# The even mixer's long convolution moved from VectorE to TensorE, and the S5 tables built in 48 steps between the weight chunks

## Chip, cores and metric

The kernel runs on one core of a Trainium2 chip. The metric is the device time of one execution in microseconds (us); less is better. Engines are TensorE (PE in the profile, its weight loads PEld), VectorE (DVE), ScalarE (ACT), GpSimd (POOL) and SyncE (SP), which here only issues transfers.

## What is computed

The reference is a network on one sequence of 512 positions with 1024 features, all in float32. A first block has an even mixer and an odd mixer, each behind a norm, and a final norm; a second block has an S5 state-space mixer, a gated unit, two MLPs and an attention. The change is in the even mixer, and in the tables which the S5 mixer uses much later:

```
p = rmsnorm(h) @ w_in
a_val, a_glu, a_gate, b_val, b_gate = split(p)
u = a_val * sigmoid(a_glu)
u = causal_depthwise_conv(u, conv_w, conv_b)
u = silu(layernorm(u))
ya = u * silu(a_gate)
yb = (multiscale_pool_diff(b_val) @ pool_w + pool_b) * pool_scale * silu(b_gate)
h = h + concat(ya, yb) @ w_out
```

The depthwise convolution has 31 taps over the positions, with weights of its own for each of the 1024 channels. The S5 tables are products of powers of a complex number for each of 64 groups by 64 states with the matrices B and C, and sines and cosines of 64 angles each.

## The kernel before

Activations lie with the features on the 128 partitions: eight tiles of 128 x 512. Weights come in chunks. `queue_w` lists them in the order of use (58 for the even mixer, 512 KB each); `prep` (line 259) loads one into one of two `raw` buffers through SP (line 264), copies it on ScalarE to `hi`, a rounded float32 (line 266), and takes the difference `lo = raw - hi` (line 268), on GpSimd if the chunk's number is in `on_pool`, which holds all numbers below 107, or else on VectorE. There are three buffers of `hi` and of `lo`, and `get_w` prepares up to three chunks ahead. `mm3` (lines 284 to 286) multiplies in three matmuls, hi by hi, hi by lo, lo by hi, so one chunk is 24 matmuls of 512 columns. `mtile` does one chunk into a PSUM bank. The elementwise helpers are recorded at one line each: `act` 225, `tt` 228, `stt` 240, `ts` 243.

`even` (line 420) runs so. The inputs are squared and split; the first four chunks multiply the input before it is normalized, while the norm is worked out (column sums, line 344; a Newton iteration on four numbers, `rsqrt_col`; a matmul that spreads them, line 373). Then for each of eight tiles `mtile` gives value and gate, and `us[c]` is value times sigmoid (as tanh). The convolution (lines 496 to 516) takes two tiles at a time in a PSUM bank each: ScalarE does the tap of one position back with the bias, VectorE the 30 others, one `stt` each over up to 512 columns, at low priority (`later(4000)`). `csum` adds up the eight results. `pooled` (line 522) and the loop behind it do the pooling half: eight chunks for values and eight for gates, with VectorE adding shifted copies. Then the mean of the convolution (a matmul of ones on `csum`, line 561), the squares, eight output chunks for the pooling half, eight chunks for the gate `a_gate` with the LayerNorm's sums and rsqrt in between (`LNC`, `LNS`: at which chunk and step), then `normed`, `gated` and `halved` for each tile and eight output chunks for the convolution half.

The S5 tables are made by the generator `tables` (line 893), eight turns, one for each `ft`; all eight are called at once at the second gated tile (`extra`, `TS = (8, 0, 0)`) at low priority (`TLATE = 8000`), so that they fill gaps. One turn has, for each half q, small products on GpSimd (line 931 on) and wide ones (`cmul`, line 955), matmuls of 128 x 32 weights on 128 columns into a quarter of a bank's partitions (lines 970, 972), transposes (line 978), copies and stores to DRAM (`tS`, `tO`, lines 982 and 989), and later `tM` (line 1001) and the sines (`reduce_angle`, `tR`, line 1017). `eng2`, which makes the output tables and the angles, is GpSimd for the first four turns and VectorE for the others.

The Tile framework orders each engine's instructions by priority in a timeline that it works out itself; `high_priority(offset)` moves some forward (`HOT = 9000` for the tables' matmuls), `later(n)` back, and `after()` binds an instruction behind the last one written for its engine. Each engine runs its instructions in order, and SP and ScalarE issue transfers from their own queues in the same order.

## Time and profile before

| | us |
|---|---|
| median of 3 runs (1898.36 to 1901.58) | 1899.34 |
| the profiled execution | 1902.89 |
| its span, first to last instruction | 1901.1 |
| TensorE busy in it | 1758.7 |
| VectorE busy in it | 1259.9 |
| ScalarE busy in it | 749.7 |
| GpSimd busy in it | 571.0 |
| even mixer: start of the span to the first matmul of the odd mixer | 446.87 |

The page cuts the span into 40 slices of 47.5 us and gives each engine's busy share in tenths. TensorE's matmuls are pipelined and the ends of their records are modelled, so a matmul's record is longer than the distance to the next one: the starts tell the pace. "x" counts records.

### The profile page before, as it was taken

The numbers are of one execution on the slowest core, as the hardware profiler recorded it, in microseconds if no ns is written. First come the engines' busy times: TensorE is split into PE (matmuls) and PEld (weight loads), VectorE is DVE, ScalarE is ACT, GpSimd is POOL, SyncE is SP. The second block draws the span as 40 slices with busy tenths as digits, with TensorE's granted clock in tenths as the row PEclk, the third lists the DMA queues.
The fourth block names the chain that finished last, engine by engine and source line by source line (L and its number), as shares of the span: only waits on it lengthen the run. The fifth ranks groups of instructions, "written<-read, shape, count | busy, mean of one in ns | idle before, by whom it ended". The sixth has DMA issues, their size and how long they took to land.

```text
span 1901.1 us, 23182 instructions
## 1 busy us (share of the span) xinstructions
PE 1758.7 (93%) x8530; PEld 1425.8 (75%) x8530; DVE 1259.9 (66%) x1940; ACT 749.7 (39%) x1274; POOL 571.0 (30%) x606
## 2 busy tenths in 40 slices
PE   6998989799988797699999999998999999999997
PEld 5776767567766676587888888887778888888886
DVE  8999999975788768844542344578776642244456
ACT  3334332443445543223432342334665542233234
POOL 4789877684556653300000000023000000000002
PEclk7999989889998998899999999999999999999998
DMA  4233233333121468723233223233111223322322
GB/s 151 78 117 99 87 106 122 110 89 102 64 75 64 125 207 297 227 78 105 100 100 95 94 100 100 92 110 113 51 44 56 93 96 100 100 91 98 100 90 93
DMA packets 104289, 200.57 MB, mean 106 GB/s; under 512 B 26736, under 2 KB 57072, under 8 KB 104176
## 3 DMA queue, kind: packets, MB, share of 16 engines
q1 hardware_dynamic: 96496, 182.41, 30.0%
q0 software_dynamic: 2640, 8.65, 1.4%
q10 hardware_dynamic: 5040, 8.04, 1.2%
q8 instruction: 67, 1.10, 0.2%
q14 instruction: 46, 0.38, 0.1%
HBM read 176.38 MB, written 22.02 MB: 104 GB/s over the span
## 4 chain that ended last, share of the span: by engine, by line
PE 57%; DVE 23%; issue 6%; DMA 5%; POOL 4%; ACT 3%; SPq 1%; ACTq 0%; DVEq 0%; POOLq 0%
PE mm L284 17%; PE mm L285 16%; PE mm L286 16%; DVE cv L240 7%; POOL lo L228 2%; DVE pl L228 1%; DMA raw<-in_w_in_odd 1%; PE pv L1519 1%; SPq L1085 1%; DVE srr L228 1%; ACT hi L225 1%; DVE e L733 1%; PE sc L284 1%; PE sc L285 1%; PE sc L286 1%
## 5 line engine op out<-in xcount | busy, mean ns | idle before, releaser
L225 ACT ACTIVATE hi<-raw 128x1024 fp32r<-128x1024 f32 (+1 forms) x280 | 292.1, 1045 | 661.3 <-PE mm L285 533.7
L228 DVE TENSOR_TENSOR lo<-raw,hi 128x1024 fp32r<-128x1024 f32 (+1 forms) x185 | 226.7, 1226 | 407.0 <-ACT hi L225 403.6
L286 PE MATMUL mm<-xg,lo 128*128 128x512 f32 x924 | 364.8, 395 | 6.4 <-POOL lo L228 6.4
L284 PE MATMUL mm<-xg,hi 128*128 128x512 f32 x924 | 365.4, 397 | 1.5 <-ACT xs L225 1.5
L285 PE MATMUL mm<-xg,hi 128*128 128x512 f32 x924 | 363.8, 395 | 0.0
L1333 POOL DMA_DIRECT2D pj<-proj x16 | 8.7, 547 | 1023.8 <-DVE t L240 784.0
L228 POOL TENSOR_TENSOR lo<-raw,hi 128x1024 fp32r<-128x1024 f32 (+1 forms) x95 | 231.3, 2436 | 134.5 <-ACT hi L225 125.1
L284 PE MATMUL mm<-hid,hi 128*128 128x512 f32 (+1 forms) x648 | 250.7, 387 | 1.8 <-DVE t L228 1.8
L285 PE MATMUL mm<-hid,hi 128*128 128x512 f32 (+1 forms) x648 | 250.3, 387 | 0.0
L286 PE MATMUL mm<-hid,lo 128*128 128x512 f32 (+1 forms) x648 | 250.1, 386 | 0.0
L286 PEld LDWEIGHTS mm<-xg,lo 128*128 128x128 f32 x924 | 175.9, 190 | 45.1 <-POOL lo L228 7.9
L284 PEld LDWEIGHTS mm<-xg,hi 128*128 128x128 f32 x924 | 176.1, 191 | 40.4 <-ACT xs L225 1.9
L285 PEld LDWEIGHTS mm<-xg,hi 128*128 128x128 f32 x924 | 175.9, 190 | 38.2 <-issue 1.2
L240 DVE SCALAR_TENSOR_TENSOR cv<-b,hw,cv 128x510 f32<-128x510 f32 (+28 forms) x232 | 158.8, 726 | 0.0
L284 PEld LDWEIGHTS mm<-hid,hi 128*128 128x128 f32 x648 | 121.7, 188 | 26.6 <-DVE t L228 2.0
L286 PEld LDWEIGHTS mm<-hid,lo 128*128 128x128 f32 x648 | 121.7, 188 | 24.7
L285 PEld LDWEIGHTS mm<-hid,hi 128*128 128x128 f32 x648 | 121.7, 188 | 24.6
L284 PE MATMUL mm<-y,hi 128*128 128x512 f32 x192 | 77.7, 405 | 10.5 <-ACT y L225 9.3
L286 PE MATMUL mm<-y,lo 128*128 128x512 f32 x192 | 75.7, 395 | 1.7 <-POOL lo L228 1.7
L285 PE MATMUL mm<-big,hi 128*128 128x512 f32 x160 | 68.5, 429 | 8.6 <-DVE big L240 7.6
L285 PE MATMUL mm<-y,hi 128*128 128x512 f32 x192 | 75.7, 394 | 0.0
L284 PE MATMUL mm<-big,hi 128*128 128x512 f32 x160 | 65.7, 429 | 10.1 <-DVE gt L240 5.8
(467 smaller groups left out, 3140.6 us busy)
## 6 DMA issues: line engine op xcount, KB each, us to landing
raw<-in_w_up SPq DMA_DIRECT2D x64, 512.0 KB
raw<-in_w_down SPq DMA_DIRECT2D x64, 512.0 KB
raw<-in_w_in_even SPq DMA_DIRECT2D x40, 512.0 KB
raw<-in_w_in_odd SPq DMA_DIRECT2D x24, 512.0 KB
raw<-in_w_out_even SPq DMA_DIRECT2D x16, 512.0 KB
raw<-in_w_glu SPq DMA_DIRECT2D x16, 512.0 KB
raw<-in_w_gate SPq DMA_DIRECT2D x16, 512.0 KB
raw<-in_w_out_odd SPq DMA_DIRECT2D x16, 384.0 KB
```

Source lines behind the costliest of these rows:

```text
L225: self.nc.scalar.activation(out=out, in_=in_, func=func, scale=scale, bias=bias)
L228: (eng or self.nc.vector).tensor_tensor(out=out, in0=a, in1=b, op=op)
L240: self.nc.vector.scalar_tensor_tensor(out=out, in0=a, scalar=s, in1=b, op0=op0, op1=op1)
L284: mm(out, hi[:, sl], xh, start=start, stop=False)
L285: mm(out, hi[:, sl], xl, start=False, stop=False)
L286: mm(out, lo[:, sl], xh, start=False, stop=stop)
L733: nc.vector.tensor_tensor_scan(out=y, data0=u[:, k], data1=x[:, k], initial=0.0, op0=ALU.mult, op1=ALU.add)
L1085: nc.sync.dma_start(out=M0[:, 128 * g:128 * g + 128], in_=bass.AP(k0.tensor, k0.offset + 4096 * g, [[16, 8], [256, 16], [1, 128]]))
L1333: self.nc.gpsimd.dma_start(out=p, in_=pj[m])
L1519: mm(o, l, r[:, w], start=n == 0, stop=n == 6 * nk - 1)
```

## The change

The convolution becomes matmuls. The channels of a tile are 16 groups of 8, and a row of positions is cut into four phases (position modulo 4). `u` is written phase by phase and stored to DRAM (`phases`), and four loads bring it back in a layout `z` that has 8 channels x 4 phases on 32 partitions, once for each of four shifts of up to three steps: 128 partitions, 16 groups of 128 columns. `taps` loads a 128 x 192 table of halved taps and spreads it, on VectorE, over the channels with a mask `own` into three 128 x 512 tiles of weights, 32 columns for each group and each of three longer shifts. `convolve` multiplies: 4 x 3 x 4 matmuls a tile, four column groups in turn, which gives 32 outputs each; ScalarE adds the bias, the result goes to DRAM and comes back with the phases in order as `conv[c]`. `step(c)` runs after tile c's gating: the sum of tile c - 4, the convolution of tile c - 3, the taps of tile c - 2; steps 8 to 11 stand in the first two pool groups.

The tables' generator now yields 48 times. `tick`, called after each weight chunk (52 times), takes one step at a small lag of priority (`TLATE = 300`), and TensorE's part of a step is put off by two ticks (`TLAG = 2`) and bound behind the chunk before it. Odd turns work on VectorE, even ones on GpSimd, the output tables always on GpSimd, the angles always on VectorE; `tS` and `tR` are stored from ScalarE's queue. The PSUM banks `tab` and `cv` become two and one. Of the even chunks' numbers from 6 to 57 the `lo` difference goes to VectorE. The norm, mean and LayerNorm steps move (`EPOS`, `MU`, `LNC`, `LNS`). The `big` tiles are taken in quarters of a four times larger tile.

```diff
-    NACT, CACT = range(8), range(0, 8, 2)
-    LNC, LNS = (6, 3), (7, 2)
-    YA, LNP, SQB, TS = 3, 2, 3, (8, 0, 0)
-    SQX, EPOS = (0, 2, 5), (0, 4)
+    MU, LNC, LNS = 2, (4, 0), (5, 0)
+    YA, LNP, SQB = 3, 2, 3
+    SQX, EPOS = (0, 2, 5), (4, 4)
+    TAPP = ()
     BOOST = 400
-    on_pool = frozenset(range(107))
+    on_pool = frozenset(n for n in range(107) if n > 57 or n % 2 or n < 6)
...
-        more(2, range(self.EPOS[0], self.EPOS[1]))
+        more(2, range(self.EPOS[0], 8))
+        more(3, range(self.EPOS[1]))
         with self.after():
             rb = self.spread_bank(rc)
...
-        us = []
+        conv, csum, ready, done = [None] * 8, self.L("b", 9), {}, []
+        def phases(c, u):
+            cu = self.dram.tile([128, T], F32, name=f"cu{c}")
+            nc.sync.dma_start(out=cu, in_=u)
+            z = self.L("big", 4, F32, (128, 4 * T)).rearrange("p (g t) -> p g t", g=16)
+            nc.gpsimd.memset(z[0:96, :, 0:3], 0.0)
+            for a in range(4):
+                src = bass.AP(cu.tensor, cu.offset, [[128, 32], [4096, 16], [1, 125 + a]])
+                nc.sync.dma_start(out=z[32 * a:32 * a + 32, :, 3 - a:128], in_=src)
+            ready[c] = z
+        def taps(c):
+            wd = self.L("wd", 2, F32, (128, 192))
+            nc.sync.dma_start(out=wd, in_=self.I["conv_a_w"][c])
+            self.act(wd, wd, AF.Copy, scale=0.5)
+            ws = []
+            for k in range(3):
+                w = self.L(*(("sq", self.SQB), ("gt", 3))[c % 2])
+                self.tt(w.rearrange("p (g d o) -> p g d o", g=16, d=8),
+                        wd[:, 64 * k:64 * k + 64].rearrange("p (g o) -> p g o", g=16).unsqueeze(2).to_broadcast([128, 16, 8, 4]),
+                        self.own.unsqueeze(1).unsqueeze(3).to_broadcast([128, 16, 8, 4]), ALU.mult, nc.gpsimd if c in self.TAPP else None)
+                ws.append(w)
+            ready[c] = ready[c], ws
+        def convolve(c):
+            z, ws = ready.pop(c)
+            y = self.bank("cv")
+            for q in range(4):
+                for k in range(3):
+                    for g in range(4):
+                        w = ws[k][:, 32 * (4 * q + g):32 * (4 * q + g) + 32]
+                        with self.after():
+                            nc.tensor.matmul(y[32 * g:32 * g + 32, 128 * q + 4 * k:128 * q + 128], w, z[:, 4 * q + g, 0:128 - 4 * k],
+                                             start=k == 0, stop=k == 2, tile_position=(0, 32 * g))
+            o = self.L("v", 2)
+            for q in range(4):
+                self.act(o[:, 128 * q:128 * q + 128], y[:, 128 * q:128 * q + 128], AF.Identity, bias=self.V("conv_a_b", 4 * c + q))
+            cy = self.dram.tile([T, 128], F32, name=f"cy{c}")
+            nc.scalar.dma_start(out=cy.rearrange("(q p) t -> p q t", p=128), in_=o.rearrange("p (q t) -> p q t", q=4))
+            conv[c] = self.L("b", 9)
+            nc.sync.dma_start(out=conv[c], in_=cy.rearrange("(h p) t -> h (p t)", p=4))
+            done.append(c)
+        def summed():
+            for c in done[len(done) - 1:]:
+                if c:
+                    self.add(csum, csum if c > 1 else conv[0], conv[c])
+        def step(c):
+            if 2 < c < 12:
+                summed()
+            if 2 < c < 11:
+                convolve(c - 3)
+            if 1 < c < 10:
+                taps(c - 2)
         for c in range(8):
             th = self.L("th", 2)
-            u = self.L("b", 9)
+            u = self.L("pl", 3)
             if c < self.EAGER:
                 pv, pg = first[2 * c:2 * c + 2]
                 self.mul(th, pg, rs)
                 pg = th
-                self.mul(u, pv, rs)
-                pv = u
+                m = self.L("v", 2)
+                self.mul(m, pv, rs)
+                pv = m
             else:
                 pv = self.mtile(xg)
+                self.tick()
                 pg = self.mtile(xg)
+                self.tick()
             self.act(th, pg, AF.Tanh, scale=0.5)
-            self.stt(u, th, 1.0, pv, ALU.add, ALU.mult)
-            us.append(u)
+            p4 = lambda x: x.rearrange("p (t o) -> p t o", o=4)
+            self.stt(u.rearrange("p (o t) -> p t o", o=4), p4(th), 1.0, p4(pv), ALU.add, ALU.mult)
+            phases(c, u)
             if c == self.EAGER - 1:
                 if self.BN == 2:
                     behind_norm()
                 extra()
-        csum = None
...
-        conv = us
+            step(c)
...
+                step(8 + 2 * g + c)
...
         for m in range(8):
             o = self.mtile(yb)
+            self.tick()
             self.add(h[m], o, h[m])
+            if m == self.MU:
+                mu = self.bank("st")
+                with self.after():
+                    nc.tensor.matmul(mu, self.ones, csum, start=True, stop=True)
+                for c in range(9):
...
         def gated(c):
-            self.mul(conv[c], conv[c], ga[c])
+            v, ga[c] = ga[c], self.L("d", 6)
+            p4 = lambda x: x.rearrange("p (t o) -> p t o", o=4)
+            self.mul(p4(ga[c]), conv[c].rearrange("p (o t) -> p t o", o=4), p4(v))
...
+        while self.behind or next(self.ft, 0) is None:
+            self.tick()
...
-    SHARED, OWN, HOT, TLATE = 4, 8, 9000, 8000
+    HOT, TLATE, TLAG = 9000, 300, 2
+    def tick(self):
+        self.ticks += 1
+        while self.behind and self.behind[0][0] <= self.ticks:
+            self.behind.pop(0)[1]()
+        if self.ft is not None:
+            with self.later(self.TLATE):
+                next(self.ft, None)
...
-            eng = nc.gpsimd if ft < self.OWN else nc.vector
-            eng2 = nc.gpsimd if ft < self.SHARED else nc.vector
+            eng, eng2 = nc.vector if ft % 2 else nc.gpsimd, nc.gpsimd
...
+                def products(q=q, wr=wr, wi=wi, cbr=cbr, cbi=cbi, kt=kt, tS=tS):
+                    if q == 0:
+                        kt.append(self.bank("tab"))
+                    for w, cb in ((wr, cbr), (wi, cbi)):
+                        for a in range(2):
+                            p4 = 2 * q + a
+                            with self.after():
+                                nc.tensor.matmul(kt[0][32 * p4:32 * p4 + 32, 0:128], cb[:, a], fl(w)[:, a], start=w is wr, stop=w is wi, tile_position=(0, 32 * p4))
+                    tp = self.bank("tab")
+                    for k, w in enumerate((wr, wi)):
+                        for a in range(2):
+                            with self.after():
+                                nc.tensor.transpose(out=tp[:, 256 * k + 128 * a:256 * k + 128 * a + 128], in_=fl(w)[:, a], identity=self.ident)
+                    sv = Q("sv", 512)
+                    nc.scalar.dma_start(out=tS.rearrange("p (k a n) -> p k a n", k=2, a=2)[:, :, q], in_=sv.rearrange("p (k n) -> p k n", k=2))
+                late(products)
+                yield
...
+                late(stored)
...
-                self.tt(ang.rearrange("p (a c) -> p a c", a=2), c3(self.chunk), s3(th8), ALU.mult, eng2)
-                r = self.reduce_angle(ang, 128, eng2, "sr")
+                self.tt(ang.rearrange("p (a c) -> p a c", a=2), c3(self.chunk), s3(th8), ALU.mult)
+                r = self.reduce_angle(ang, 128, None, "sr")
...
+                nc.scalar.dma_start(out=tR.rearrange("p (k a n) -> p k a n", k=2, a=2)[:, :, q], in_=rt)
+                yield
...
-        with self.phase(mm=4, tab=1, cv=2):
+        with self.phase(mm=4, tab=2, cv=1):
```

Two small unused tiles (`pad`, `gap`) shift later addresses in SBUF.

## Rows read from the trace of the kernel before

**Rows 1.** The page: an engine's busy time, one engine's slices, the chain.
```profile
PE 1758.7 (93%) x8530; PEld 1425.8 (75%) x8530; DVE 1259.9 (66%) x1940; ACT 749.7 (39%) x1274; POOL 571.0 (30%) x606
...
DVE  8999999975788768844542344578776642244456
...
PE 57%; DVE 23%; issue 6%; DMA 5%; POOL 4%; ACT 3%; SPq 1%; ACTq 0%; DVEq 0%; POOLq 0%
PE mm L284 17%; PE mm L285 16%; PE mm L286 16%; DVE cv L240 7%; POOL lo L228 2%; DVE pl L228 1%; DMA raw<-in_w_in_odd 1%; PE pv L1519 1%; SPq L1085 1%; DVE srr L228 1%; ACT hi L225 1%; DVE e L733 1%; PE sc L284 1%; PE sc L285 1%; PE sc L286 1%
```

**Rows 2.** Sums by stage: busy us (records) of each engine, clock, DMA share, GB/s.
```profile
725.00:750.00 25.00, 17.84 (x170) 14.66 (x170) 21.77 (x38) 7.58 (x11) 13.73 (x11) 0.77 0.99 356
0.00:447.00 447.00, 386.40 (x1675) 299.30 (x1676) 422.28 (x723) 169.93 (x350) 339.69 (x440) 0.93 0.35 108
...
55.00:447.00 392.00, 346.90 (x1516) 267.87 (x1515) 374.51 (x578) 149.40 (x312) 313.52 (x402) 0.94 0.34 104
```

**Rows 3.** TensorE's timeline: start, duration, line, what it multiplies, shapes.
```profile
54.85 0.63 PE L284 MATMUL mm<-xg,hi 128*128 128x512 f32 x2
...
352.80 0.39 PE L284 MATMUL mm<-xg,hi 128*128 128x512 f32 x1
...
358.26 0.39 PE L284 MATMUL mm<-xg,hi 128*128 128x512 f32 x1
...
386.50 0.42 PE L970 MATMUL tab<-tq_wr,cbr 128*32 128x128 f32 x4 [0.37 <-ACT tq_kq L225]
386.72 0.42 PE L972 MATMUL tab<-tq_wi,cbi 128*32 128x128 f32 x4
...
446.87 0.47 PE L284 MATMUL mm<-xg,hi 128*128 128x512 f32 x1
```

**Rows 4.** TensorE's waits, 50 to 450 us: total, times, longest (14 entries).
```profile
PE st L561 <- DVE b L228: 6.4, 1, 6.4
PE st L373 <- DVE rs_s L240: 6.0, 1, 6.0
PE mm L284 <- DVE gt L240: 5.8, 1, 5.8
PE tab L996 <- ACT tq_sv L225: 4.9, 4, 1.9
```

**Rows 5.** VectorE, 0 to 447 us: instructions on tiles cv, srr and srk, in turn.
```profile
0.00:447.00 447.00, 164.23 (x240) 0.93 0.35 108
...
0.00:447.00 447.00, 23.04 (x32) 0.93 0.35 108
...
0.00:447.00 447.00, 14.91 (x40) 0.93 0.35 108
```

**Rows 6.** VectorE by line and shape: 0 to 447, last row 447 to 900.
```profile
L228 DVE TENSOR_TENSOR d<-v,d 128x512 fp32r<-128x512 f32 x8 | 14.1, 1758 | 0.0
...
L228 DVE TENSOR_TENSOR h<-mm,h 128x512 f32<-128x512 f32 x16 | 10.8, 681 | 4.9 <-PE mm L286 4.9
...
L228 DVE TENSOR_TENSOR tq_wi<-tq_wi,tq_u 128x256 f32<-128x256 f32 x8 | 6.0, 754 | 0.1
...
L228 DVE TENSOR_TENSOR tq_ang<-ctile,sbr 128x128 f32<-128x128 f32 x8 | 2.7, 338 | 1.1 <-ACT tq_rt L225 1.1
...
L228 DVE TENSOR_TENSOR lo<-raw,hi 128x1024 fp32r<-128x1024 f32 x21 | 25.6, 1222 | 44.2 <-ACT hi L225 44.1
```

**Rows 7.** GpSimd by line and shape, 0 to 415 us.
```profile
L228 POOL TENSOR_TENSOR lo<-raw,hi 128x1024 fp32r<-128x1024 f32 x55 | 135.0, 2456 | 62.4 <-ACT hi L225 60.6 <-issue 1.6
L228 POOL TENSOR_TENSOR tq_wi<-tq_wi,tq_u 128x256 f32<-128x256 f32 x23 | 20.1, 875 | 0.7
```

**Rows 8.** SP: issue (ns min/median/max), its wait; transfers: count, size, landing.
```profile
L989 SPq DMA_DIRECT2D tO<-tq_wr x32: 577/600/642, 86.8 to 444.0; - x32
...
SPq L264 <- POOL lo L228: 166.6, 41, 15.4
...
U<-du POOLq DMA_DIRECT2D x8, 256.0 KB, 4.7
```

More of the change, by code (lines that the diff above doesn't have):

```diff
@@ L136, in host_layout @@
     c.add("half", np.repeat(np.repeat(np.eye(2, dtype=np.float32)[::-1], 64, axis=0), 16, axis=1))
+    c.add("own", np.tile(np.repeat(np.eye(8, dtype=np.float32), 4, axis=0), (4, 1)))
     c.add("not0", np.repeat((np.arange(64) > 0).astype(np.float32)[None], 128, axis=0))
@@ L173, in __init__ @@
         self.p_s = P("small", 4)
+        P("pad", 1).tile([128, 16], F32, name="pad")
         self.p_raw = P("raw", 2)
@@ L404, in consts @@
         self.tab, self.U, self.acc12 = [], [], []
+        self.ft, self.behind, self.ticks = None, [], 0
     def load_x(self, ps=None):
@@ L431, in even @@
                 self.act(q, h[k], AF.Square)
-            xu.append(self.split(h[k], self.LR("big", 16), self.V("g_even", k)))
+            xu.append(self.split(h[k], [self.quarter() for _ in range(2)], self.V("g_even", k)))
             if k == 0:
@@ L467, in even @@
             self.act(rs, rb, AF.Copy)
-        more(2, range(self.EPOS[1], 8))
-        more(3, range(8))
+        more(3, range(self.EPOS[1], 8))
         xg = []
@@ L590, in even @@
                     self.mm3(pg, w, k, xg[k], k == 0, k == 7)
-            g = self.L("big", 16)
+            self.tick()
+            g = self.quarter(F32)
             self.act(g, pg, AF.Silu)
@@ L609, in even @@
                         f(k)
-        tables(2)
         n = self.YA
@@ L898, in tables @@
         nc.gpsimd.memset(z, 0.0)
-        cbr, cbi = (self.L(n, 1, F32, (128, 2, 32)) for n in ("cbr", "cbi"))
-        nc.gpsimd.memset(cbr, 0.0)
-        nc.gpsimd.memset(cbi, 0.0)
+        cbs = [[self.L(f"cb{n}{q}", 1, F32, (128, 2, 32)) for n in "ri"] for q in range(2)]
+        for cb in cbs:
+            for t in cb:
+                nc.gpsimd.memset(t, 0.0)
         cr, ci, pr, pi, m8, th8 = small
@@ L960, in cmul @@
                     self.tt(out, out, u, op, eng)
-                wr, wi = F("wr", 2), F("wi", 2)
+                wr, wi = F("wr", 3), F("wi", 3)
                 cmul(wr, pw(pr, 0), hb(bbr), pw(pi, 0), hb(bbi), ALU.subtract, eng)
                 cmul(wi, pw(pr, 0), hb(bbi), pw(pi, 0), hb(bbr), ALU.add, eng)
-                for a in range(2):
-                    p4 = 2 * q + a
-                    o = kt[32 * p4:32 * p4 + 32, 0:128]
-                    with self.tc.high_priority(offset=self.HOT):
-                        nc.tensor.matmul(o, cbr[:, a], fl(wr)[:, a], start=True, stop=False, tile_position=(0, 32 * p4))
-                    with self.tc.high_priority(offset=self.HOT):
-                        nc.tensor.matmul(o, cbi[:, a], fl(wi)[:, a], start=False, stop=True, tile_position=(0, 32 * p4))
@@ new lines, in tables, with inside, turned @@
+                late(stored)
+                if q == 1:
+                    def inside(ft=ft, kt=kt, tM=tM):
+                        ks = Q("ks", 128)
+                        self.act(ks, kt[0][:, 0:128], AF.Copy)
+                        self.stt(ks[:, 0:16], self.eye16, dg[:, ft:ft + 1], ks[:, 0:16], ALU.mult, ALU.add)
+                        def turned():
+                            kp = self.bank("tab")
+                            with self.after():
+                                nc.tensor.transpose(out=kp[:, 0:128], in_=ks, identity=self.ident)
+                            kq = Q("kq", 128)
+                            self.act(kq, kp[:, 0:128], AF.Copy)
+                            for j in range(8):
+                                nc.sync.dma_start(out=tM[:, :, 8 + j].rearrange("g h m -> h g m"), in_=kq[16 * j:16 * j + 16].rearrange("p (g m) -> p g m", g=8))
+                        self.behind.insert(0, (self.ticks + 1, turned))
+                    late(inside)
@@ L1685, in behind_norm @@
                         self.small = next(small)
-            def tables(i):
-                if on("s5"):
-                    with self.later(self.TLATE if i == 0 else 0), self.after(mybir.EngineType.DVE) if i else nullcontext():
-                        for _ in range(self.TS[i]):
-                            next(self.ft)
-            h = self.even(h, behind_norm, extra, tables)
+            h = self.even(h, behind_norm, extra)
         if on("odd"):
```

139 lines of the change are left out of this document (50 added, 89 removed).

## The prediction

> **What bounds the kernel now.** I read the page first, from its engine line to its slices and its chain [rows 1]. TensorE is busy for 93% of the span, but VectorE's slices stand at 8 or 9 through the first eight of forty, and nowhere later for so long. In the chain of waits 23% is VectorE, and the largest VectorE entry, 7%, is the convolution line. So the even mixer, the first quarter, is a stage in which VectorE paces TensorE. The sums by stage say it in time [rows 2]: from 0 to 447 us VectorE is busy for 422 us, TensorE's records cover 386, GpSimd 340, ScalarE 170. Outside the even mixer the change touches nothing, so only this stage counts.
>
> Then the pace of TensorE itself. Its timeline [rows 3] has the first matmul on normalized activations at 54.85 and the first of the odd mixer at 446.87: 392 us. At full clock 24 matmuls, one weight chunk, go from 352.80 to 358.26: 5.46 us. Of the 58 chunks of queue_even four are done before 54.85, so 54 x 5.46 = 295 us are dense matmuls and 392 - 295 = 97 us are something else. The list of TensorE's waits [rows 4] has 14 entries between 50 and 450, 45 us in all; the rows show the three longest, which are the LayerNorm sum, the rsqrt behind it and a pool gate, all owed by VectorE, then the first of six entries for the S5 tables, which together take 17.6 us. About 19 us more are the small matmuls of tables and norms (estimate: sixteen half tables, each with eight product records in two rounds of 0.22 us [rows 3] and transposes for as long again, and 5 us for the norms). The other 33 us are matmuls at the lower clock, which follow each stop: granted clock 0.94 over 55 to 447 [rows 2].
>
> **The change, part by part.** *Convolution off VectorE.* Its 240 instructions are 164 us of VectorE [rows 5]. All go.
>
> *Convolution onto TensorE.* Per tile 4 x 3 x 4 = 48 matmuls in F32, K = 128, 32 columns of weights, 120 to 128 columns of data; 384 in all. The nearest rows are the table products, of the very same shape [rows 3]: each matmul leaves two records, and at 386.50 four records, two matmuls in different column groups, are through in 0.22 us, when the next four begin. The change puts four groups side by side. If all four share as the two do, a tile is 12 x 0.22 = 2.6 us and the sum 21; if only pairs share, 42; if each ran alone, 84, which the rows exclude for two groups. I take 21, since in the rows the second group costs nothing beside the first, and keep 42 as the upper end. The Trainium skill, TensorEngine Tiling (Array Packing), Theoretical Speedup, gives weights of up to 32 columns up to four times the speed; by it too the sum would be 21.
>
> *What feeds it.* Per tile VectorE gains three 512-wide tensor_tensor that spread the taps. Bounds: 0.68 us, the add on a PSUM operand that never meets GpSimd, and 1.76 us, the same size on SBUF while GpSimd works [rows 6]; I take 0.9, as GpSimd will be less busy: 24 x 0.9 = 22 us. ScalarE gains some 20 us of bias and scaling on 170 busy of 447, hidden in its gaps. GpSimd gains eight small memsets, hidden likewise. SP gains seven transfers a tile, 56 x about 0.6 us of issue [rows 8], but gives the 32 stores of tS and tR to ScalarE's queue, at the same price 19 us there, still within ScalarE's idle time. The bytes are 1.9 MB a tile, 15 MB in all, beside 108 GB/s x 447 us = 48 MB now; from 725 to 750 us the core moved 356 GB/s [rows 2]. Each step of the convolution uses what was stored at least a tile earlier, some 11 us of dense matmuls, so I cost latency at nothing; the cover is the three-tile lag.
>
> *Weight halves.* 26 of the even chunks' subtractions move from GpSimd, 2.46 us each [rows 7], to VectorE, 1.22 us as in the odd mixer [rows 6]: +32 us VectorE, -64 GpSimd.
>
> *Tables.* All angle reductions go to VectorE: the eight it does now cost 23.0 + 14.9 + 2.7 = 41 us [rows 5, 6], so +41. Of the output tables it gives up 48 operations of 256 columns, at most 0.75 us and at least the 0.34 of a 128-wide product [rows 6]; I take 0.6, so -29. For odd tiles it takes over 8 x (6 small at 0.3 and 6 wide at 0.6) = 43 us, with four pairs that scale B 46. GpSimd sheds these at 0.88 for a wide one [rows 7], 8 x (6 x 0.3 + 6 x 0.88) = 57 us; the angles it sheds and the output tables it gains are about equal.
>
> *Order.* The table steps lose the early place that HOT gave their matmuls, and the convolution's products come between them. Their 64 stores of tO and 64 of tM stay on SP, in the same number, those of tO two ticks later, so that SP no longer stands before an unfinished one; the weight loads behind them gain by that. At the start the column sums of the first norm move behind four more steps of 3 matmuls, 2.7 us, and as many fewer follow them: between 3 us lost, if rsqrt sets the end of the first norm, and 3 gained, if the eight steps now cover it; I take nothing. The mean moves behind the third output tile and the LayerNorm's rsqrt to gate chunks 4 and 5, so three chunks, 16 us, cover the normalizing instead of three quarters of one.
>
> *Sum on VectorE:* 422 - 164 + 22 + 32 + 41 - 29 + 46 = 370 us, and less as GpSimd falls from 340 to some 220 and holds it up less often: 345 to 370. That is below the 390 us at which TensorE can end at best (54.85 + 295 + 19 + 21). **TensorE becomes the bound.**
>
> *What is regained.* The wait for the LayerNorm sum goes, since the convolution ends in the second pool group, some 25 chunks earlier. The gate wait goes with VectorE's queue. Of the rsqrt wait (6.0 us, now covered by one chunk) I keep 3. Of the tables' 17.6 I keep 4: their matmuls now stand in TensorE's order two ticks, 11 us, behind the vector work. With 5 for weights, 12 of 45 us stay. The low-clock part shrinks alike, 33 to 9. The odd mixer starts without table work beside it: 3. In all 33 + 24 + 3 = 60 us back. Paid: 21 for the convolution and 10 for new waits of TensorE in its now fixed order (bounds 0 and 17.6, what tables cost today; taken near the middle). Behind a late product stands every dense matmul, as nothing may pass it. Net -29 us.
>
> The profiled execution took 1902.9 us (span 1901.1); the median of the runs is 1899.3, 3.6 less. 1902.9 - 29 = 1874, and by the median **1870 us**.
>
> **The rivals.**
> - *Cleaner than I think:* all waits go and only the floor of 390 us stays: 447 - 390 = 57 back, 1843. Against it: VectorE at 345 to 370 of 390 leaves little slack. 7%.
> - *Pairs only:* the four groups share two by two: 21 us more, 1891. For it: no row has more than two groups. 11%.
> - *VectorE remains the bound:* its new tensor_tensor pay contended prices, taps 24 x 1.76 = 42 and halves 26 x 1.9 = 50, so 408 us; with the 25 us of idling that it has now, 433: 14 back, 1885. It decides if GpSimd stays above some 300 us. 8%.
> - *Not the convolution:* the waits come from weights and queues; only sum, gate and rsqrt go, 18 us and 13 of slow clock, which the 31 paid eat up: 1899. Against it: weights are not among the long waits of TensorE [rows 4]. 5%.
> - *Slower, by SP's queue:* SP is in order. For each tile it must wait until u has landed in DRAM before it may issue the four loads, and again until the convolution's output has landed; a 256 KB transfer that reads DRAM back takes 4.7 us elsewhere [rows 8]. The weight loads stand behind. If a hold, store and issue together, reaches 9 us (two such landings), it outruns the 5.46 us of one chunk in reserve by 3.5, sixteen times: 56 us lost, 27 slower, 1926. It decides when a hold exceeds about one chunk. Against it: SP already waits 167 us for free raw buffers [rows 8], so loads run ahead. 9%. The Trainium skill, DMA: Bandwidth & Descriptors, Specifications, says that pieces under 512 B cause a read-modify-write; three of the four loads have pieces of 500 to 508 B, and no row here prices that; by it the holds would be longer.
>
> **How the numbers follow.** The forecast has 60%. Its own range is 1856 to 1884, from 0 or 17.6 us of new waits and from half of the kept 12 + 9 either way. 8 in 10 asks for the pair case on one side and the floor on the other: 1843 to 1894; what stays out is the fourth and fifth rival and the forecast's own tails. A measurement can tell about 0.2%, 3.8 us, from no change. Faster by more: forecast, floor, VectorE case and most of pairs, 84%; within: the fourth rival and the edge of pairs, 6%; slower: 10%.
>
> **What would show it.** Right: the first odd matmul near 418; no wait on the LayerNorm sum; convolution visits of 2.6 us; VectorE 345 to 370 us; GpSimd near 220. Wrong: visits of 5 us (pairs), VectorE at 100% until the end with TensorE waiting for it, or TensorE waiting for weights whose loads sat in SP behind the loads of the shifted copies.

## The result

| | median us | range | runs |
|---|---|---|---|
| before | 1898.85 | 1897.41 to 1901.58 | 4 |
| after | 1886.58 | 1885.77 to 1887.84 | 4 |

The ratio is 0.993 (95% interval 0.9918 to 0.9943): faster by 12.3 us, where 29 were forecast. The profiled execution of after took 1886.16 us, span 1884.3.

The page of after, with the rows that answer to [rows 1]: VectorE has lost 93 us, the chain's share of it falls from 23% to 14%, and the convolution is gone from the chain.

```profile
PE 1764.2 (94%) x9298; PEld 1439.7 (76%) x9298; DVE 1167.2 (62%) x1885; ACT 762.0 (40%) x1330; POOL 456.6 (24%) x422
...
DVE  9989777555888859655432344578686642244456
...
PE 68%; DVE 14%; issue 5%; POOL 4%; ACT 4%; DMA 3%; SPq 1%; ACTq 0%; DVEq 0%; POOLq 0%
```

The sums by stage, as in [rows 2], the first up to the first odd matmul:

```profile
0.00:425.72 425.72, 386.61 (x2443) 309.84 (x2443) 329.52 (x666) 180.26 (x405) 223.03 (x255) 0.95 0.53 149
...
55.00:200.00 145.00, 122.06 (x1214) 98.59 (x1213) 127.17 (x302) 56.24 (x157) 76.97 (x101) 0.92 0.81 199
200.00:300.00 100.00, 97.73 (x462) 78.03 (x462) 71.74 (x97) 44.28 (x101) 64.37 (x72) 1.00 0.39 122
300.00:425.00 125.00, 124.52 (x596) 100.49 (x595) 80.17 (x108) 55.01 (x96) 56.90 (x52) 1.00 0.36 113
```

From 200 us on TensorE hardly stops. Most of what it still loses behind the first norm lies between 55 and 200, at a granted clock of 0.92. TensorE's timeline there and at the end, as in [rows 3]: a visit of the convolution (six of the eight take 2.75 us), one of the two that had to wait (4.76 and 3.99), the first odd matmul.

```profile
101.58 2.75 PE L534 MATMUL cv<-big,gt 128*32 128x128 f32 x96
...
163.54 4.76 PE L534 MATMUL cv<-big,gt 128*32 128x128 f32 x96 [5.52 <-ACT v L249]
...
425.72 0.39 PE L308 MATMUL mm<-xg,hi 128*128 128x512 f32 x1
```

TensorE's waits from 50 to 450 us, as in [rows 4]: 10 entries, 26.5 us in all, where before had 45. The LayerNorm sum, the rsqrt and VectorE's late gate are gone. New are the convolution's one PSUM bank, which ScalarE empties late, and one low half on VectorE.

```profile
PE cv L534 <- ACT v L249: 11.4, 3, 5.5
PE mm L310 <- DVE lo L252: 8.1, 2, 7.4
PE tab L1085 <- DVE tq_ks L264: 2.5, 1, 2.5
PE tab L1051 <- POOL tq_wr L252: 1.6, 1, 1.6
...
PE mm L308 <- ACT hi L249: 0.4, 1, 0.4
```

Where the lead was made and lost: 21.2 us at the first odd matmul (446.87 to 425.72), 19.6 at the first product of the S5 stage behind the odd mixer (735.5 to 715.9, the first start in each row below), 16.8 at the end of the span.

```profile
L1161 PE MATMUL sp<-U,x x256: 222/222/369, 735.5 to 798.3; 128*64 128x64 f32 x128
```
```profile
L1251 PE MATMUL sp<-U,x x256: 222/222/369, 715.9 to 779.4; 128*64 128x64 f32 x128
```

So 1.6 us go in the odd mixer, where TensorE's waits for the high halves `wrh` grow from 6.6 us (before, 447 to 665) to 10.5 (after, 425 to 645). The other 2.8 go in the stages behind it; what takes them stays open.

```profile
PE sp L284 <- ACT wrh L225: 6.6, 2, 4.4
```
```profile
PE sp L308 <- ACT wrh L249: 10.5, 3, 6.1
```

Another 4.5 are between the profiled executions and the medians: the profiled execution of before (1902.89) took longer than any of its four timed runs, that of after (1886.16) stands 0.4 below its median.

### The profile page after: what moved, and what is told of

It is laid out like the page before. It is cut to its first block, busy times and chain, and to the rows that moved or that the text cites. A ratio compares the mean times of both kernels' runs of the same rounds, so it can differ in the third digit from the quotient of the medians.

```text
span 1884.3 us, 24650 instructions
## 1 busy us (share of the span) xinstructions
PE 1764.2 (94%) x9298; PEld 1439.7 (76%) x9298; DVE 1167.2 (62%) x1885; ACT 762.0 (40%) x1330; POOL 456.6 (24%) x422
## 4 chain that ended last, share of the span: by engine, by line
PE 68%; DVE 14%; issue 5%; POOL 4%; ACT 4%; DMA 3%; SPq 1%; ACTq 0%; DVEq 0%; POOLq 0%
PE mm L308 19%; PE mm L310 19%; PE mm L309 19%; POOL lo L252 2%; DVE lo L252 1%; DVE e L808 1%; ACT hi L249 1%; PE pv L1609 1%; SPq L1175 1%; PE sc L309 1%; PE sc L308 1%; PE sc L310 1%; DVE pl L264 1%; DVE srm L267 1%; DVE h L264 1%
## 5 line engine op out<-in xcount | busy, mean ns | idle before, releaser
L252 DVE TENSOR_TENSOR lo<-raw,hi 128x1024 fp32r<-128x1024 f32 (+1 forms) x211 | 262.1, 1243 | 422.1 <-ACT hi L249 417.3
L310 PE MATMUL mm<-xg,lo 128*128 128x512 f32 x924 | 361.0, 391 | 9.4 <-DVE lo L252 8.1
L308 PEld LDWEIGHTS mm<-xg,hi 128*128 128x128 f32 x924 | 173.8, 188 | 44.9 <-ACT hi L249 2.3
L252 POOL TENSOR_TENSOR lo<-raw,hi 128x1024 fp32r<-128x1024 f32 (+1 forms) x69 | 170.6, 2473 | 146.8 <-ACT hi L249 140.6
L309 PEld LDWEIGHTS mm<-xg,hi 128*128 128x128 f32 x924 | 173.8, 188 | 36.4 <-DVE xg L252 1.4
L309 PE MATMUL mm<-big,hi 128*128 128x512 f32 x160 | 64.5, 403 | 3.9 <-DVE big L264 3.9
L308 PE MATMUL mm<-big,hi 128*128 128x512 f32 x160 | 65.3, 411 | 2.2 <-ACT hi L249 2.2
L310 PE MATMUL mm<-big,lo 128*128 128x512 f32 x160 | 64.2, 402 | 0.1
```

What stands on the lines that cost most here:

```text
L252: (eng or self.nc.vector).tensor_tensor(out=out, in0=a, in1=b, op=op)
L308: mm(out, hi[:, sl], xh, start=start, stop=False)
L309: mm(out, hi[:, sl], xl, start=False, stop=False)
L310: mm(out, lo[:, sl], xh, start=False, stop=stop)
```

## The experiments

All ratios are to the kernel before on the same chip; after stands at 0.993. "First odd" is the first odd matmul of the profiled run (after: 425.7). The instruction order is worked out anew for every edit, so a few us can come from that alone; e13 below shows nearly 6.

**What the convolution, the tables' products and the copies cost.**

*e2.* The gated tiles take the convolution's place; `phases`, `taps` and `convolve` are not called.

```diff
-            u = self.L("pl", 3)
+            u = conv[c] = self.L("b", 9)
...
-            phases(c, u)
+            done.append(c)
+            summed()
...
-            step(c)
...
-                step(8 + 2 * g + c)
```


> Leaves the long convolution out: no shifted copies, no taps, no matmuls, no bias; the gated tiles go into the sum as they are. The tables stay in their 48 steps. It measures all that the convolution costs in its new place. Its 8 visits of 2.75 us and the three slow ones are 25 us of TensorE. Theory (the convolution costs TensorE little more than its own matmuls, the tables cost the stops): the first odd matmul at 388 to 398, 28 to 38 us earlier than 425.7, with waits for table products and weight halves still there. Rival (the copies through DRAM and the taps are what stops the stretch): 25 us of matmuls, 26 of waits and 12 of low clock all go, first odd matmul at or before 365.

Measured: 1862.9 us (one run), first odd 403.6, 22.1 us earlier: as much as eight visits of 2.75 us. The stops stayed, under other names: 7.5 us for low halves on VectorE, 4.5 on GpSimd, 4.8 for high halves. The theory asked for 28 to 38 us and gets less, but its reading holds: the convolution costs TensorE little more than its own matmuls. The rival (365 or before) falls.

*e3.* No table step before the last chunk.

```diff
-    HOT, TLATE, TLAG = 9000, 300, 2
+    HOT, TLATE, TLAG, T0 = 9000, 300, 2, 52
...
-        if self.ft is not None:
+        if self.ft is not None and self.ticks > self.T0:
```


> No table step runs during the even mixer; all 48 come behind its last chunk in one lump, so the whole is slower and only the marks up to the last dense matmul of the even mixer (425 now) count. The convolution stays as it is. Theory (the tables' vector work, at one step a chunk, makes the stops): besides their 16 to 19 us of small matmuls, 15 to 25 us of waits and some 8 of low clock go, last dense matmul of the even mixer at 378 to 390. Rival (the convolution's feed is at fault): only their own small matmuls go, 406 to 411.

The whole took 1978.8 us (one run). The last dense matmul of the even mixer comes at 398.0 instead of 425.5, between the theory (378 to 390) and the rival (406 to 411). The LayerNorm's mean, further ahead, comes at 276.5 instead of 300.0. Up to there the table matmuls of after have 13.7 us, so about 10 us of stops went with them. The angle chains did not wait for the lump: 45 of their 48 `srm` operations still ran between 50 and 200 us, since nothing but one buffer holds them. So this run does not price the angles.

*e4.* One shifted copy for all tiles.

```diff
+        zs = []
...
         def phases(c, u):
...
+            if c:
+                ready[c] = zs[0]
+                return
...
+            zs.append(z)
```


> The shifted copies are stored, cleared and loaded for tile 0 alone and serve all eight tiles: 7 of 8 stores of u and 28 of 32 loads of 250 KB are left out, so the output is not the convolution's from tile 1 on. All matmuls, taps and table steps stay. Theory (transfers are not the limit): at most 4 us less than 1886.6. Rival (the DMA share of 0.81 between 55 and 200 us, or SP holding the weight loads behind these loads, is the limit): 20 to 30 us less, 1857 to 1867, with the first odd matmul before 405.

Ratio 0.9943 (0.9925 to 0.9961), 1891.2 us; first odd 433.4. The DMA share between 55 and 200 us fell from 0.81 to 0.45 and the time did not fall; TensorE's wait for the convolution's bank rose to 20.8 us. The theory holds: transfers are not the limit.

**ScalarE's and VectorE's order.** After's ScalarE stands 63 us in front of sines that VectorE owes, and 15 of the 16 angle chains run between 50 and 200 us. My first theory was that this crowding stops TensorE.

*e1.* Sines one step later.

```diff
-                self.act(ang, r, AF.Abs)
...
+                self.behind.insert(0, (self.ticks + 1, sines))
```


> The sines of a table step (absolute value, two sines, their store on ScalarE's queue) stand one step later in the program, with a second buffer for the angles; nothing else moves. Theory (ScalarE, in order, stops in front of a sine that VectorE still owes, 63 us in all, and behind it stand the high halves of the weights and the reads that empty the one convolution bank): those waits shrink from 63 us to under 20, TensorE's waits for the convolution bank from 11.4 us to under 4, the first odd matmul comes at 410 to 416 instead of 425.7, and the time is 10 to 16 us less, 1871 to 1877. Rival (ScalarE's stops lie beside work that is late anyway: VectorE, or the transfers, pace the stretch): under 2 us, 1884 to 1888.

Ratio 0.9894 (0.9877 to 0.9911), first odd 422.4: some 3 to 7 us, short of the theory's 10 to 16, although ScalarE's waits for VectorE's angles fell from 63 us to 10; the bank's wait only went from 11.4 to 10.5.

*e5.* Angle chains held in their steps; *e7* adds e1 and puts the S5 vectors behind the last output tile; *e12* runs one chain every second step with e1, S5 vectors in the pool groups; *e17* moves the S5 vectors alone.

```diff
-                self.tt(ang.rearrange("p (a c) -> p a c", a=2), c3(self.chunk), s3(th8), ALU.mult)
+                with self.after(mybir.EngineType.DVE):
+                    self.tt(ang.rearrange("p (a c) -> p a c", a=2), c3(self.chunk), s3(th8), ALU.mult)
```


> Only the first operation of each angle chain is bound in order behind the last VectorE instruction of its own step; nothing is added or taken away. In the changed kernel all 16 chains, whose steps reach to the last gate chunks, were issued by 190 us, 58 us of VectorE's 127 busy between 55 and 200. Theory (the chains run early and crowd VectorE in the stretch in which taps, weight halves and the S5 vectors also fall; ScalarE's and TensorE's stops follow from that): VectorE between 55 and 200 falls to 85 to 100 us, ScalarE's wait for sines from 63 us to under 30, the first odd matmul comes at 405 to 414 instead of 425.7, the time is 11 to 18 us less than 1886.6. Rival (it does not matter when the chains run; the one convolution bank, the weight halves or the S5 vectors stop TensorE): under 4 us.

> Three moves of order together: the angle chains held in their steps, their sines one step behind them, and the 45 small operations for the S5 vectors of the odd mixer put behind the last output tile of the even mixer instead of at the start. Theory: besides what holding the chains gives, the 7.4 us wait for one low half at 72 to 80 us, behind which those vectors stood, goes, and ScalarE's stops for sines go: first odd matmul at 398 to 408, time 1860 to 1870. Rival (each of these covers the next wait): no better than the held chains alone.

> Order alone: one angle chain every second step from the start, bound to that step, so that the 16 end near 290 us, between the changed kernel's 190 and the held chains' 420; the sines one step behind; the S5 vectors of the odd mixer in the pool groups. Theory (VectorE has to be evenly filled, at about 77% of 55 to 425, and then covers): VectorE 105 to 112 of 145 between 55 and 200 and 70 to 78 of 100 from 200 to 300, TensorE's waits from 50 to 450 under 15 us, first odd matmul at 405 to 415, time 1866 to 1876. Rival (each order only moves the stop): 1882 to 1890.

> Of the changed kernel only the 45 small operations for the S5 vectors move, from behind the second tile to the second pool group. Theory (they hold the one late half at 72 to 80 us, 7.4 us of TensorE's 26.5): that wait goes, first odd matmul at 418 to 423, time 3 to 8 us less. Rival (each removed stop is taken by the next): under 2 us.

Measured: e5 0.9927 (0.9911 to 0.9944), e7 0.9927 (0.991 to 0.9944), e12 0.9892 (0.9875 to 0.9908), e17 0.9915 (0.9896 to 0.9933); first odd 428.1, 426.0, 424.9, 424.4. In e7 the stretch itself got better, 136 us of TensorE in 145 instead of 122, and the gain was lost behind it. The stages of e7 (columns as above):

```profile
55.00:200.00 145.00, 136.34 (x1286) 109.64 (x1285) 100.74 (x169) 54.24 (x140) 90.68 (x113) 0.96 0.79 202
200.00:425.00 225.00, 210.95 (x983) 168.85 (x982) 177.90 (x338) 99.43 (x214) 115.32 (x111) 0.97 0.39 116
```

The LayerNorm's rsqrt, now among angle chains and S5 vectors on VectorE, made TensorE wait 8.9 us. No theory's first odd matmul came. The rivals hold for e5, e7 and e12: order moves the stops. e17 lies between its two (1.3 us at the first odd matmul, some 3 by the ratio): the wait for low halves on VectorE falls from 8.1 us to 4.9, and the bank's grows from 11.4 to 13.0.

*e9.* Of each chain only the product and the clamp stay.

```diff
-                r = self.reduce_angle(ang, 128, None, "sr")
+                r = self.L("srr", 1, F32, (128, 128))
+                self.ts(r, ang, 3.1415925, ALU.min, -3.1415925, ALU.max)
```


> Leaves out the range reduction of the table angles: of each chain's 14 operations of 128 columns only the product and the last clamp stay, so the sines get clamped angles and the S5 tables are not the reference's. The sines on ScalarE, their stores, the convolution, the halves and every place in the program stay. VectorE is 46 to 55 us lighter, nearly all of it between 55 and 200 us, where it is busy 127 of 145. Theory (VectorE's crowding in that stretch is what holds TensorE, since leaving out the convolution or the transfers took no stop away): VectorE between 55 and 200 at 75 to 90, first odd matmul at 400 to 410 instead of 425.7, time 1864 to 1874. Rival (the stops come from orders and single buffers, whoever is busy): under 6 us, 1881 or more.

VectorE is 32 us lighter up to the first odd matmul (297.3 instead of 329.5), not 46 to 55: a chain has 10 operations, not the 14 that the expectations of e9 and e6 say, and 8 of them go. Its stretch:

```profile
55.00:200.00 145.00, 130.16 (x1258) 104.65 (x1258) 98.69 (x186) 57.16 (x155) 80.99 (x106) 0.94 0.82 201
```

First odd 420.2, ratio 0.9867 (0.9852 to 0.9881): 5.5 us for 32, the rival's under 6 and not the theory's 15 to 25, though the time fell by more, some 8 to 12 us. VectorE's load is not the main cause. *e6* asks the same by giving the chains to GpSimd.

```diff
-                self.tt(ang.rearrange("p (a c) -> p a c", a=2), c3(self.chunk), s3(th8), ALU.mult)
-                r = self.reduce_angle(ang, 128, None, "sr")
+                self.tt(ang.rearrange("p (a c) -> p a c", a=2), c3(self.chunk), s3(th8), ALU.mult, eng2)
+                r = self.reduce_angle(ang, 128, eng2, "sr")
```


> All angle chains run on GpSimd instead of VectorE, 16 x 14 operations of 128 columns; their place in the program is as in the changed kernel. VectorE loses some 65 us, GpSimd gains some 100 at the 0.3 to 0.46 us that it paid before. Theory (VectorE's crowding between 55 and 200 is the cause): TensorE's waits for halves on VectorE go and the first odd matmul comes at 408 to 418; but the table products on GpSimd stand behind the chains now, so TensorE's waits for tq_wr grow by up to 10 us. Time 1872 to 1886. Rival (VectorE's load is not the cause): 1887 or more.

Ratio 0.9982 (0.9966 to 0.9997), first odd 439.6: VectorE lost 40 us (289.7), and TensorE came 14 us later. A lighter VectorE alone doesn't help; GpSimd, now busy for 302.8 us instead of 223.0, is a second change of this run.

**The weight halves.** Only `on_pool` changes, the numbers of the chunks whose low half is made on GpSimd:

```diff
-    on_pool = frozenset(n for n in range(107) if n > 57 or n % 2 or n < 6)
+    on_pool = frozenset(range(107))
...
+    on_pool = frozenset(n for n in range(107) if n > 57)
...
+    on_pool = frozenset(n for n in range(107) if n > 57 or n % 2 and n >= 6)
...
+    on_pool = frozenset(n for n in range(107) if n > 57 or n < 6)
...
+    on_pool = frozenset()
```

In this order e8, e11, e13, e14 and e16. e10 is the kernel before with after's set. The edits do more than two expectations say: e11 moves 32 halves, not 26, since it takes the first six chunks along, and e13 moves all of those six, not three.

> The 26 subtractions of weight halves that the change gave to VectorE go back to GpSimd, 35 us less on VectorE in the even mixer, 11 of them between 55 and 200, and some 60 more on GpSimd (223 of 425 us now). Theory (they are a small part of the crowding): 0 to 6 us less. Rival (their place on VectorE, behind vector chains, makes the late halves and with them most of the stops): 10 to 20 us less, and no wait of TensorE for a low half above 2 us.

> The kernel before, with nothing changed but that the 26 weight-half subtractions go from GpSimd to VectorE as in the change. VectorE, busy 422 of 447 us there, gains 26 x 1.2 to 1.4 = 31 to 36 us, GpSimd loses some 64. Theory (in the kernel before VectorE paces the even mixer, so this part alone does not pay; the part pays in the changed kernel only because the convolution left VectorE): 5 to 30 us slower, 1904 to 1930. Rival (the slow subtractions on GpSimd are a cost of their own, also before): 5 to 15 us faster.

> The changed kernel with all weight halves of the even mixer on VectorE, 26 more than the change moved: VectorE +32 to 35 us (330 to about 364 of 425), GpSimd 223 to about 165. Giving back the first 26 cost 14 us, so if the price is GpSimd's slow halves and what they do to VectorE's operations beside them, the second 26 gain again: 4 to 12 us faster, 1875 to 1883. If VectorE's crowding is the limit, they cost: 3 to 15 us slower, 1890 to 1902, with the loss between 55 and 200 us. I hold the second for likelier, since VectorE has 18 us of 145 free there.

> The changed kernel with the first three even chunks of the six at the start moved from GpSimd to VectorE, and of chunks 6 to 57 the odd ones left on GpSimd as they were. The first six halves stand beside VectorE's busiest stretch (50 of 55 us) and in front of the first norm's column sums. If the gain of all halves on VectorE came from the start, the first matmul on normalized activations comes some 5 us earlier than 51.2 and the first odd matmul at 418 to 421, 4 to 7 us faster in all. If it came from the steady state, both move by less than 3 us.

> The changed kernel with all of chunks 6 to 57 on VectorE and the first six left on GpSimd. If a half on GpSimd costs VectorE about as much as it would take itself (VectorE busy 327.5, 329.5 and 329.0 us with 0, 26 and 58 halves on it), the total on VectorE stays within 325 to 335, and the stops between 55 and 200 shrink: first odd matmul at 414 to 418, 7 to 12 us faster. If the start gave it all, less than 3 us.

> All weight halves of the whole kernel on VectorE, also those of the odd mixer and the S5 stage up to chunk 106, where TensorE waits 11 us for halves from GpSimd between 425 and 645 (POOL lo and wrl). Theory (the same price there): 5 to 12 us faster than with the even halves alone, ratio 0.974 to 0.979. Rival (VectorE paces the S5 stage): the odd mixer gains, S5 loses, 0.981 or above.

| | on GpSimd | on VectorE | VectorE busy | without halves | first odd | ratio |
|---|---|---|---|---|---|---|
| e8 | 60 | 0 | 336.7 | 336.7 | 444.6 | 1.0008 (0.9998 to 1.0018) |
| after | 34 | 26 | 329.5 | 294.2 | 425.7 | 0.993 (0.9918 to 0.9943) |
| e14 | 8 | 52 | 323.3 | 256.4 | 413.9 | 0.9828 (0.9811 to 0.9845) |
| e11 | 2 | 58 | 318.9 | 245.6 | 409.8 | 0.9811 (0.9797 to 0.9826) |

Counts and busy times are up to the first odd matmul of each run, in which all four did the same work (2443 weight loads of TensorE and, halves apart, 640 instructions of VectorE). The figures in e14's expectation are cut at 425 us in every run and so hold different work. The sums of e8 and of e11:

```profile
0.00:444.59 444.59, 396.61 (x2442) 315.08 (x2443) 336.70 (x640) 179.76 (x405) 278.72 (x281) 0.95 0.51 143
```
```profile
0.00:409.78 409.78, 387.50 (x2443) 311.00 (x2443) 318.89 (x698) 180.24 (x405) 154.91 (x223) 0.97 0.55 155
```

"Without halves" takes off the line of VectorE's own subtractions; e11's row of it, and the one for GpSimd in e8, which is 150 us:

```profile
L252 DVE TENSOR_TENSOR lo<-raw,hi 128x1024 fp32r<-128x1024 f32 x58 | 73.3, 1263 | 29.7 <-ACT hi L249 29.5
```
```profile
L252 POOL TENSOR_TENSOR lo<-raw,hi 128x1024 fp32r<-128x1024 f32 x60 | 150.0, 2501 | 89.9 <-ACT hi L249 78.8 <-PE mm L309 4.8 <-DMA raw<-in_w_out_even 3.6
```

58 fewer halves on GpSimd take 91 us off VectorE's other work, 1.57 us each. A half that GpSimd makes costs VectorE more than the 1.26 us for which VectorE makes it itself. The timelines of VectorE and GpSimd in after show one such case: an operation of 12 columns, whose neighbours of the same kind take 0.15 to 0.72 us, starts 0.12 us behind a half on GpSimd and ends with it.

```profile
72.00 0.58 DVE L264 SCALAR_TENSOR_TENSOR sv_xs_p<-sv_xs_p,sv_xs_r 128x12 f32<-128x12 f32 x1
...
72.64 2.30 DVE L264 SCALAR_TENSOR_TENSOR sv_su<-sv_xs_p,sv_xs_i 128x12 f32<-128x12 f32 x1
```
```profile
72.52 2.40 POOL L252 TENSOR_TENSOR lo<-raw,hi 128x1024 fp32r<-128x1024 f32 x1
```

In e11, with no half beside it, the same operation takes 0.61:

```profile
66.28 0.61 DVE L264 SCALAR_TENSOR_TENSOR sv_su<-sv_xs_p,sv_xs_i 128x12 f32<-128x12 f32 x1
```

Nor does every operation of VectorE pay. Two `stt` of one shape, eight of each, in e8 and then in e11: the one that reads two tiles in SBUF takes 1590 ns and 788, the one that reads its first operand in PSUM 743 and 740.

```profile
L264 DVE SCALAR_TENSOR_TENSOR big<-gt,vecs,big 128x512 fp32r<-128x512 f32 x8 | 12.7, 1590 | 0.2
...
L264 DVE SCALAR_TENSOR_TENSOR gt<-mm,vecs,gt 128x512 f32<-128x512 f32 x8 | 5.9, 743 | 3.5 <-PE mm L310 3.5
```
```profile
L264 DVE SCALAR_TENSOR_TENSOR big<-gt,vecs,big 128x512 fp32r<-128x512 f32 x8 | 6.1, 788 | 0.1
L264 DVE SCALAR_TENSOR_TENSOR gt<-mm,vecs,gt 128x512 f32<-128x512 f32 x8 | 5.9, 740 | 0.0
```

The Trainium skill, SBUF — State Buffer, Who interferes with whom, says that a VectorE instruction with two SBUF inputs contends with a GpSimd instruction that reads SBUF; these rows agree. The 7.4 us wait of TensorE at 72 us is partly this: the late low half, on VectorE at 77.8, stood behind that chain.

What follows: the change without its halves (e8) is no faster than the kernel before, where its theory and its rival both had it faster than after, and the halves without the convolution's move (e10: 1.0065, 1.0046 to 1.0084) are slower. Only together do they gain. e10 is slower as its theory has it, but not by the theory's way: VectorE did not gain 31 to 36 us, it lost 4 (417.7 instead of 422.1), 40 of its other work against 36 for the 26 halves, so a half on GpSimd costs it 1.55 us there too. What grew are TensorE's waits in front of the tables' matmuls, from 17.6 us to 33.5, while its others fell from 27 to 24:

```profile
PE tab L970 <- POOL tq_wr L228: 14.9, 6, 10.9
```

TensorE's waits from its first matmul on normalized activations to the first odd one go with the halves on GpSimd: 36 us in e8, 26 in after, 16 in e14 and in e11. By which way is not shown. VectorE's other instructions get shorter, but with the same edit GpSimd gets 124 us lighter from e8 to e11 and each half takes 1.24 us less, and no run moves one of the three alone. That VectorE is lighter in all is not enough: 18 us less from e8 to e11 go with a first odd matmul 35 us earlier, 32 less in e9 with 5.5.

e13, 0.9887 (0.9867 to 0.9907): the first matmul on normalized activations comes at 43.2 instead of 51.2, but the first odd at 423.4, so behind the start 5.7 us are lost with the same halves as in after, and neither branch of the expectation holds. e14: 11.8 us of the 16 belong to the steady state; it gains more than expected (17 to 19 us, not 7 to 12). e16: 0.9668 (0.9649 to 0.9687); its first odd matmul is only 2.6 us ahead of e11, but the MLP's first matmul on `hid` is 32 us ahead (915.95 against 948.23), more than its theory asked for. So the same cost runs through the odd mixer and S5: from the first odd matmul to that mark VectorE's work without halves is 317 us in e11 and 270 in e16. TensorE's waits for halves there were these in after (425 to 645 us), 7.5 and 2.4 us, and the time lost beside them was larger:

```profile
PE yp L310 <- POOL lo L252: 7.5, 6, 2.7
...
PE sp L310 <- POOL lo L252: 2.4, 2, 1.5
```

I expected e11 to be slower, as VectorE had 18 us free in the stretch. VectorE did not get fuller.

**Both together.** e15 is e11 with e1; e18 is e16 with e12's order.

> All even halves on VectorE and the sines one step later, the two orders that gained most alone (16 and 3 us of the even mixer). Theory (two separate stops): first odd matmul at 403 to 408, ratio to the kernel before 0.976 to 0.980. Rival (VectorE is full between 55 and 200, 131 of 145, so ScalarE's place no longer counts): 0.981 as with the halves alone.

> No weight half on GpSimd in the whole kernel, and the order of the paced run: angle chains every second step, sines a step later, S5 vectors in the pool groups. In the changed kernel the pacing gained 3 to 7 us by the ratio. Theory (VectorE between 55 and 200, 130 of 145, still stops TensorE for 17 us): 4 to 10 us faster than without halves alone, ratio 0.961 to 0.965. Rival (moved stops): 0.966 to 0.969.

e15 0.9841 (0.9823 to 0.9858), e18 0.9711 (0.9693 to 0.9729): neither beats the kernel it builds on, and both come out above their rivals' ratios. e16, one line away from after, is the best: by the ratios some 50 us faster than after, more than 60 faster than before. What is left in its stretch (128 us of TensorE in 145) no order tried here gave back; that stays open.

## Why the prediction was wrong, point by point

*Right.* The visits of the convolution: 2.6 forecast, 2.75 measured, so four column groups share as the table products' two did, and the pairs rival is out; by e2 the sum is 22 us, 21 forecast. The Trainium skill, TensorEngine Tiling (Array Packing), Theoretical Speedup, gives weights of up to 32 columns up to four times the speed; the 2.75 us for 48 matmuls agree. The latency of the copies costs nothing (e4), so the rival by SP's queue is out: SP's waits for u in DRAM and for the output, up to 427 us, hold it for 5.5 us at most, some 7 with the four issues behind it (estimate, 0.48 us each), not the 9 from which that rival decides (as in [rows 8]). One hold that it did not name is longer, 11.3 us before the load of a table of taps. TensorE waited no more than 0.4 us for a high half between 50 and 450 us all the same.

```profile
SPq L515 <- DVE sq L252: 11.3, 1, 11.3
SPq L510 <- DMA cu<-pl: 9.7, 4, 5.5
...
SPq L542 <- DMA cy<-v: 6.8, 2, 5.5
```

The waits for the LayerNorm's sum, the rsqrt and the gate went as said. GpSimd came to 223 (some 220), and without the halves' term the sum on VectorE, 338, is what e8 has, 337.

*VectorE: 330, forecast 345 to 370.* The term that failed is "weight halves: +32 us VectorE". Its own price is near (26 x 1.36 = 35), though the 1.22 us are not from the odd mixer: in before VectorE makes no half from 447 to 700 us. But e8 has 337 without them and after 330 with them: the net is -7. The sum let GpSimd hold VectorE up "less often" as one lump; it is 1.57 us for each half.

*What is regained: the step that failed* ("In all 33 + 24 + 3 = 60 us back"). It put the gain on the convolution's leaving (60 regained, 31 paid) and no gain of time on the halves. With the halves left on GpSimd, e8 shows that the convolution, the tables and the new order by themselves give 0; with them, 12.3. The 32 halves of the even mixer left on GpSimd cost up to 16 us more there (e11), which the sum had as "5 for weights".

*The sum against the trace.* Measured between the first normalized matmul and the first odd one: 425.7 - 51.2 = 374.5, less 295 dense, 22 convolution and 19 small matmuls as forecast, leaves 38.5, of which 26.5 are waits and so 12 low clock. By the prediction's terms: TensorE's waits fell by 18.4 us with the new ones counted (23 forecast, 33 back less 10), the low clock gave 21 (24), the convolution cost 22 (21), and the first norm, costed at nothing, gave 3.7. The new waits came in order, as feared, behind ScalarE's sines and VectorE's chains. So the even mixer missed by 5 us (425.7 against 421 before the 3 us put into the odd mixer); without the norm's 3.7, which is luck, it would be 8.5. The odd mixer was to give 3 and lost 1.6: 4.6 us. Behind it 2.8 more were lost, where the prediction said that the change touches nothing. The rest, 4.4, is that I took the profiled run of before as 3.6 above its median and the profiled run of after is not. No single term is the whole miss of 16.6 us; with all even halves on VectorE (e11, ratio 0.981) the kernel passes the forecast (1870 of 1899.3, 0.985).

*The rivals.* "VectorE remains the bound" has the time (1885) and not the mechanism: it wanted VectorE at 408 us and GpSimd above 300; they had 330 and 223. "Not the convolution" came nearest in kind, though it spoke of queues; and its price for the rest, nothing gained, is what e8 has. It is the halves' engine, which TensorE's waits in before name with 4.6 us only (the same list as [rows 4]), while part of the cost falls on VectorE's other instructions:

```profile
PE mm L286 <- POOL lo L228: 4.6, 2, 2.6
```

## What to carry to other kernels

When work moves between GpSimd and VectorE, price what it does to the other engine's instructions beside it, not only its own rows: compare a small operation's usual time with its time beside a long GpSimd one. A wait list names who was late, not who made him late. When one edit has several parts, leave each out alone early; here without the smallest, one line, the rest gained nothing, and it pointed to a gain four times as large.

## What the hardware showed that I had not expected

A subtraction of 128 x 1024 on GpSimd (2.5 us) took 1.57 us from VectorE in the mean of the even mixer, more than VectorE's own 1.26 for the same work, and an operation of one shape doubled (1590 ns against 788) with both tiles in SBUF and stayed (743 against 740) with one in PSUM. And 28 loads of some 250 KB from DRAM, with pieces of 500 to 512 bytes, could be left out without any gain (e4), at a DMA share of 0.81 in their stretch.
